# A recurrent layer's input projection as seven block products for eight, with the residual kept in DRAM

## The chip, the cores and the metric

The kernel runs on one core of a Trainium2 chip. The metric is the device time of one execution in microseconds (us). The time before is the median of three runs, 1123.8 us.

## The reference

Two pre-norm residual layers and a final RMSNorm over x of shape (1, 1024, 1024), all in float32. Layer 0 is a gated linear recurrence, layer 1 an attention with forget gates; the change touches layer 0 alone.

```python
h = rms_norm(x, norm_g[0])
u = h @ w_in                                  # (1024, 1024) @ (1024, 3072)
xb, gate = u[..., :1536], u[..., 1536:]
xc = causal_depthwise_conv(xb, conv_w, conv_b)        # 4 taps
r = sigmoid(block_diag_linear(xc, wa, ba))            # 12 blocks of 128 x 128
i = sigmoid(block_diag_linear(xc, wx, bx))
log_a = -8 * r * softplus(-a_param); a = exp(log_a)
hs = scan(a, sqrt(1 - a**2) * i * xc)                 # h[t] = a[t] h[t-1] + b[t]
x = x + (hs * silu(gate)) @ w_out                     # (1024, 1536) @ (1536, 1024)
# layer 1 (attention), then rms_norm
```

## The kernel before

Everything lies transposed: features on the 128 partitions, the 1024 positions along the free axis, cut into two halves of 512 (`halves`, index h). The model's 1024 features are eight blocks of 128 (k), and the recurrence's width of 1536 is twelve blocks (n). Each float32 operand of a product is split into a high part (`to_hi`, L85 or L87) and a low part, the rest (`to_lo`, L96), and each product of two blocks is three matmuls of 128x128 by 128x512: high by high, low by high, high by low (`gemm_steps`, all recorded at L54).

Layer 0 walks over the twelve blocks n. For each it needs two projections, `ups` (the value branch, weights `w0[n]`) and `gps` (the gate branch, weights `w0[12 + n]`), and each of these is eight blocks k by two halves h by three matmuls, so 48 matmuls and 96 for the pair. The split input lives in `raw[h][k]` throughout. The norm's reciprocal `rs` is multiplied in afterwards (L289, L323). Behind the projections come, for block n:

- `conv` (L289, L290, L293): `us` from PSUM, one ScalarE pass and three taps on VectorE, then the split of the result.
- `gates` (L314): 12 matmuls and four tanh on ScalarE.
- `silu` (L323 to L325) on `gps`; the projection of the gate branch and its silu run one block behind the value branch.
- `recur` (L339 to L348): tanh, exp, square and square root on ScalarE, a scan on VectorE (L348).
- `outputs` (L356): the product with the gate branch, and its split into `yh`, `yl`.

`project_out(g)` takes blocks 2g and 2g+1 back to the model's width: 16 results (8 feature blocks by 2 halves) of 6 matmuls each. VectorE adds each result from PSUM to the residual x, which is held in 16 SBUF tiles (L381). These results are the `fill`: the loop hands them out between the projections, four at a time. The last of the six groups runs after the loop, where each sum goes on at once into squares, into layer 1's split input (L247) and to DRAM as `x1d` (L475).

A scheduler orders the instructions of each engine at build time from this program; on the chip every engine then runs its own list strictly in that order, and so a waiting instruction holds up all that are behind it on its engine. PSUM has eight banks: the tag "S" has two slots of two banks (an `ups` or a `gps`), the tags "g" (results of the output projection) and "O" (gates) have two of one bank. Weights come in pieces of four blocks (256 KB) on SyncE's DMA queue through three `wf` buffers and one of four takes `wx`; the split weights have four `wh` and four `wl` buffers.

## Time and profile before

| | us |
|---|---|
| runs | 1123.17, 1123.8, 1128.24 |
| median | 1123.8 |
| span of the profiled execution | 1127.7 |
| TensorE matmuls busy | 1114.3 (99%) |
| VectorE, ScalarE, GpSimd busy | 758.6, 589.3, 195.6 |

The times do not mark which run the profile was taken from. Only 1128.24 can hold a span of 1127.7, so it is read as the profiled execution's own time: 0.5 us lie around the span.

The profile's page gives busy times by engine, the span in 40 slices, the chain of work that ended last, and groups of like instructions; further views give the same by stage or in order of time. PE is TensorE's matmuls, PEld its weight loads, DVE is VectorE, ACT is ScalarE, POOL is GpSimd, SP is SyncE. A matmul's recorded duration overlaps with that of its neighbours. The granted TensorE clock is given as a share of full speed.

### The profile page before, as it was taken

The page shows a single profiled execution, that of the slowest core. Times are in us where ns is not written, and L with a number is a line of the kernel's source. Part 1 is how long each engine was busy: PE and PEld are TensorE (multiplying, and loading weights), DVE is VectorE, ACT ScalarE, POOL GpSimd, SP SyncE. Part 2 cuts the span into 40 slices and gives each one's busy share as a digit, 9 for nine tenths or more (in the row PEclk, how much of TensorE's full clock was granted, in tenths as well). Part 3 has the DMA queues.
Part 4 walks back from the last instruction along what each step waited for, and adds up shares of the span by engine and source line. Part 5 has one row for each costly group of instructions (what it writes and reads, how often), then busy time and mean ns, then how long its engine had stood idle before and what let it go on. Part 6 is the DMA issues. An engine that isn't in the chain of part 4 may idle for free.

```text
span 1127.7 us, 15774 instructions
## 1 busy us (share of the span) xinstructions
PE 1114.3 (99%) x5691; PEld 936.8 (83%) x5691; DVE 758.6 (67%) x1268; ACT 589.3 (52%) x1081; POOL 195.6 (17%) x155
## 2 busy tenths in 40 slices
PE   9999999999999999999999999999999999999997
PEld 7788888888888887988888988889888898888786
DVE  7888755776568789656676466664667646676545
ACT  8488345355453656365555355553555535644335
POOL 1322112221121201431021110212102110021220
PEclk9999999999999999999999999999999999999999
DMA  6111111111111114433425224242252422564345
GB/s 235 57 47 42 51 52 52 38 58 45 52 38 52 47 44 145 129 112 102 112 71 123 66 77 117 72 118 71 74 119 73 118 71 77 176 189 158 117 154 187
DMA packets 62902, 105.43 MB, mean 93 GB/s; under 512 B 9796, under 2 KB 24772, under 8 KB 62824
## 3 DMA queue, kind: packets, MB, share of 16 engines
q1 hardware_dynamic: 59704, 95.97, 28.9%
q0 software_dynamic: 3120, 8.46, 2.3%
q8 instruction: 45, 0.74, 0.3%
q14 instruction: 33, 0.27, 0.1%
HBM read 63.30 MB, written 15.93 MB: 70 GB/s over the span
## 4 chain that ended last, share of the span: by engine, by line
PE 92%; DMA 2%; DVE 2%; issue 1%; ACT 1%; SPq 1%; POOL 0%; DVEq 0%; POOLq 0%; ACTq 0%
PE gps L54 33%; PE ops L54 16%; PE ups L54 12%; PE vps L54 8%; PE S L54 6%; PE O L54 6%; PE pt L58 5%; PE gate L54 3%; PE turn L54 3%; DMA wf<-in_wo 1%; DMA x<-in_xt 1%; POOL wl L96 0%; PE rsrow L54 0%; DMA wf<-in_w 0%; DMA yhl<-y1d 0%
## 5 line engine op out<-in xcount | busy, mean ns | idle before, releaser
L54 PE MATMUL gps<-hh,wh 128*128 128x512 f32 x576 | 229.1, 398 | 0.6 <-DVE qkl L595 0.6
L54 PE MATMUL gps<-hh,wl 128*128 128x512 f32 x576 | 226.8, 394 | 0.0
L54 PE MATMUL gps<-hl,wh 128*128 128x512 f32 x576 | 226.7, 394 | 0.0
L85 ACT CAST wh<-wf 128x512 fp32r<-128x512 f32 (+2 forms) x156 | 94.2, 607 | 147.8 <-PE ops L54 55.3
L96 POOL TENSOR_TENSOR wl<-wf,wh 128x512 fp32r<-128x512 f32 (+1 forms) x60 | 101.0, 1689 | 389.8 <-ACT wh L85 362.5
L720 ACT ACTIVATE p<-S,m 128x128 f32<-128x128 f32 (+7 forms) x128 | 94.8, 741 | 137.9 <-DVE m L715 136.8
L96 DVE TENSOR_TENSOR pl<-pt,ph 128x512 fp32r<-128x512 f32 (+1 forms) x198 | 98.7, 540 | 88.1 <-ACT ph L85 87.6
L54 PEld LDWEIGHTS gps<-hl,wh 128*128 128x128 f32 x576 | 108.3, 188 | 24.7 <-issue 0.5
L54 PEld LDWEIGHTS gps<-hh,wh 128*128 128x128 f32 x576 | 108.6, 189 | 20.5 <-DVE qkl L595 0.8
L54 PEld LDWEIGHTS gps<-hh,wl 128*128 128x128 f32 x576 | 108.7, 189 | 20.1 <-POOL wl L96 0.6
L715 DVE CUSTOM_DVE_ANT_0 S<-S,mask 128x128 f32<-128x128 f32 (+7 forms) x128 | 97.3, 761 | 28.8 <-PE S L54 28.8
L85 ACT CAST ph<-pt 128x512 fp32r<-128x512 f32 (+1 forms) x198 | 83.6, 473 | 36.2 <-PE pt L58 28.9
L54 PE MATMUL S<-T,U 96*128 96x512 f32 (+7 forms) x384 | 91.9, 348 | 2.7 <-ACT p L720 2.7
L96 DVE TENSOR_TENSOR wl<-wf,wh 128x512 fp32r<-128x512 f32 x96 | 70.7, 741 | 28.3 <-ACT wh L85 27.4
L381 DVE TENSOR_TENSOR x<-x,ops 128x512 f32<-128x512 f32 x80 | 54.1, 683 | 48.0 <-PE ops L54 48.0
L54 PEld LDWEIGHTS S<-T,U 128*128 128x128 f32 (+1 forms) x384 | 68.6, 190 | 16.1 <-ACT p L720 3.5
L58 PE MATMUL pt<-ident,p 128*128 128x128 f32 x576 | 79.4, 273 | 0.8 <-DVE pl L96 0.5
L58 PEld LDWEIGHTS pt<-ident,p 128*128 128x128 f32 x576 | 67.2, 140 | 13.9 <-issue 2.9
L54 PE MATMUL ups<-hh,wh 128*128 128x512 f32 x192 | 76.1, 397 | 1.1 <-ACT hh L87 1.1
L54 PE MATMUL ups<-hl,wh 128*128 128x512 f32 x192 | 76.7, 399 | 0.2
L54 PE MATMUL ops<-yh,wh 128*128 128x512 f32 x192 | 76.0, 396 | 0.5 <-DVE x L474 0.5
L54 PE MATMUL ups<-hh,wl 128*128 128x512 f32 x192 | 76.2, 397 | 0.0
(183 smaller groups left out, 2247.8 us busy)
## 6 DMA issues: line engine op xcount, KB each, us to landing
wf<-in_w SPq DMA_DIRECT2D x100, 256.0 KB
wf<-in_wo SPq DMA_DIRECT2D x64, 128.0 KB
U<-qkh SPq DMA_DIRECT2D x64, 128.0 KB
T<-qkh SPq DMA_DIRECT2D x28, 256.0 KB
x<-in_xt SPq DMA_DIRECT2D x16, 256.0 KB
x1d<-x SPq DMA_DIRECT2D x16, 256.0 KB
wf<-in_wv SPq DMA_DIRECT2D x16, 256.0 KB
U<-qkl SPq DMA_DIRECT2D x32, 128.0 KB
```

What stands on the lines that cost most here:

```text
L54: pe[0] = nc.tensor.matmul(*args, **kw)
L58: pe[0] = nc.tensor.transpose(*args)
L85: nc.scalar.copy(hi, src)
L96: return eng.tensor_tensor(lo, src, f32(hi), ALU.subtract)
L381: nc.vector.tensor_tensor(x, x, pt, ALU.add)
L715: nc.vector.tensor_tensor_reduce(S[:, :n], S[:, :n], mask[:, SEQ - n :], -1.0, -NEG, ALU.add, ALU.min, accum_out=m)
L720: seen[0] = nc.scalar.activation(p, S[:, :n], AF.Exp, bias=m, scale=-1.0, accum_out=sums[:, i : i + 1])
```

## The change

Blocks n = 3 to 11 no longer multiply eight times. With the two projections as the rows of a 2 by 2 block matrix (a11, a12 of `ups`, a21, a22 of `gps`, each half of the eight k) and the input's halves of k and of the positions as another, seven products of sums (12 matmuls each) take the place of eight, in a form of Strassen's scheme. The sums of the input (`other_sums`) are formed once, at n = 1 and 2, out of the x tiles, which they overwrite; the sums of the weights (`sums_of_weights`) are formed for each block on GpSimd. Three copies or sums pass between the PSUM banks on VectorE and ScalarE (`products`). Blocks 0 to 2 keep the eight products.

As the x tiles are consumed, x is copied from its input to `x1d` in DRAM at n = 2, and each result of the output projection is copied by ScalarE to an SBUF tile `o` (four buffers, shared with two tiles of `products`) and added to `x1d` by a DMA that GpSimd issues. After the loop the 16 x tiles are loaded again from `x1d`. The silu of a block now follows its own conv, the second gate's tanh comes first and is multiplied by `xc` in `gates`, `us` stays in PSUM, and several tiles have one buffer for two. The order of the fill is written out (`pace`). The scratch memory for DMA descriptors is set to 2048.

```diff
-GROUP = 2
+OUTS = 4
+PLAIN = 3
...
-        if spare and next(loads) % 4 == 3:
-            return spare[0].tile([P, *shape], F32, tag="wx", name="wf")
...
-        ypool = l0.enter_context(pool("y", 2 * GROUP))
+        early_x = l0.enter_context(ExitStack())
+        xpool = early_x.enter_context(pool("x", 1))
...
+        def split_pair(pair_, src, lo_eng):
+            hi, lo = pair_
+            to_hi(hi, src, nc.scalar)
+            to_lo(lo, src, hi, lo_eng)
+            return pair_
+        quad = {}
+        def other_sums(ks):
+            for k in ks:
+                lo_, hi_ = (gnt[:, 0, j : j + 1] for j in (k, k + 4))
+                t2, t3, n1, t4 = xs[0][k], xs[1][k + 4], xs[1][k], xs[0][k + 4]
+                nc.scalar.activation(t3, t3, AF.Copy, scale=hi_)
+                nc.scalar.activation(t2, t2, AF.Copy, scale=lo_)
+                stt = nc.vector.scalar_tensor_tensor
+                stt(t3, n1, lo_, t3, ALU.mult, ALU.subtract)
+                stt(n1, n1, lo_, t2, ALU.mult, ALU.subtract)
+                nc.vector.tensor_tensor(t2, t3, t2, ALU.subtract)
+                stt(t4, t4, hi_, t2, ALU.mult, ALU.add)
+                for key, src, eng in (("t2", t2, nc.vector), ("t3", t3, nc.gpsimd), ("n1", n1, nc.gpsimd), ("t4", t4, nc.gpsimd)):
+                    if key == "t4":
+                        to = pair()
+                    else:
+                        to = tuple(
+                            tpool.tile([P, HALF], F32R, tag=v, name=v, bufs=12) for v in ("th", "tl")
+                        )
+                    quad.setdefault(key, []).append(split_pair(to, src, eng))
+        def sums_of_weights(n):
+            def raw_w(block, k, tag, pool_=tmp):
+                wt = loaded([4, P]) if tag == "wf" else pool_.tile([P, 4, P], F32, tag=tag, name=tag, bufs=2)
+                nc.sync.dma_start(wt, w0[block][:, k : k + 4])
+                return wt
+            def split(src, lo_eng):
+                hi = wpool.tile([P, 4, P], F32R, tag="wh", name="wh")
+                lo = wpool.tile([P, 4, P], F32R, tag="wl", name="wl")
+                to_hi(hi, src, nc.scalar)
+                to_lo(lo, src, hi, lo_eng)
+                return [(hi[:, k], lo[:, k]) for k in range(4)]
+            def add(o, a, b):
+                nc.gpsimd.tensor_tensor(o, a, b, ALU.add)
+            a21, a22 = raw_w(NB + n, 0, "wx"), raw_w(NB + n, 4, "wx")
+            a11 = raw_w(n, 0, "wf")
+            s1, s2 = (tmp.tile([P, 4, P], F32, tag="ws", name="ws", bufs=2) for _ in range(2))
+            add(s1, a21, a22)
+            add(s2, s1, a11)
+            yield split(s2, nc.vector)
+            add(a21, a21, a11)
+            yield split(a21, nc.gpsimd)
+            yield split(a11, nc.gpsimd)
+            yield split(s1, nc.vector)
+            yield split(a22, nc.gpsimd)
+            a12 = raw_w(n, 4, "wf")
+            add(s2, s2, a12)
+            yield split(a12, nc.gpsimd)
+            yield split(s2, nc.vector)
+        def partial_sums(o, w, x, start):
+            for k, ((wh, wl), (xh, xl)) in enumerate(zip(w, x)):
+                for i, (a, b) in enumerate(((wh, xh), (wl, xh), (wh, xl))):
+                    matmul(o, a, b, start=start and k == i == 0, stop=k == 3 and i == 2, skip_group_check=not start)
+        def products(n, ups, gps):
+            sets = sums_of_weights(n)
+            p1, q5, q7, q6 = ups[:, 0], ups[:, 1], gps[:, 0], gps[:, 1]
+            w_, v5 = (ypool.tile([P, HALF], F32, tag="o", name=v, bufs=OUTS) for v in ("wk", "vk"))
+            tt = nc.vector.tensor_tensor
+            partial_sums(q6, next(sets), quad["t2"], True)
+            yield
+            partial_sums(q7, next(sets), quad["t3"], True)
+            yield
+            partial_sums(p1, next(sets), raw[0][:4], True)
+            nc.scalar.copy(w_, p1)
+            tt(w_, w_, q6, ALU.add)
+            tt(q7, q7, w_, ALU.subtract)
+            yield
+            partial_sums(q5, next(sets), quad["n1"], True)
+            nc.scalar.copy(v5, q5)
+            tt(q5, w_, q5, ALU.subtract)
+            tt(q6, q7, v5, ALU.add)
+            yield
+            partial_sums(q7, next(sets), quad["t4"], False)
+            yield
+            partial_sums(p1, next(sets), raw[0][4:], False)
+            yield
+            partial_sums(q5, next(sets), raw[1][4:], False)
+        def product(pt, h, w, ks=range(KT)):
+            gemm(pt, [(w[k], raw[h][k]) for k in ks])
 
         def conv(n, ups):
-            us, xc = long("us"), long("xc", bufs=2)
-            for pt, cs in zip(ups, halves if len(ups) == 2 else (slice(0, SEQ),)):
-                nc.vector.tensor_tensor(us[:, cs], pt, rs[:, cs], ALU.mult)
+            xc = long("xc")
+            if isinstance(ups, list):
+                us = long("m2")
+                for pt, cs in zip(ups, halves):
+                    nc.vector.tensor_tensor(us[:, cs], pt, rs[:, cs], ALU.mult)
+            else:
+                us = ups.rearrange("p a b -> p (a b)")
+                nc.vector.tensor_tensor(us, us, rs, ALU.mult)
             nc.scalar.activation(xc, us, AF.Identity, bias=cb[:, n : n + 1], scale=cw[3][:, n : n + 1])
...
-            for j, b_ in enumerate((hba, hbx)):
+            th, ti = s["t"] = long("th"), long("ti")
+            for j, b_ in ((1, hbx), (0, hba)):
+                if j:
+                    nc.vector.scalar_tensor_tensor(ti, ti, 1.0, s["xc"], ALU.add, ALU.mult)
...
+        def silu(s, gps):
             gs = gps.rearrange("p a b -> p (a b)")
-            sg = s["sg"] = long("sg")
-            for cs in parts:
-                g_, s_ = gs[:, cs], sg[:, cs]
-                nc.vector.tensor_tensor(g_, g_, rs[:, cs], ALU.mult)
-                nc.scalar.activation(s_, g_, AF.Tanh, scale=0.5)
-                nc.vector.scalar_tensor_tensor(s_, s_, 1.0, g_, ALU.add, ALU.mult)
-                yield
+            sg = s["sg"] = tmp.tile([P, SEQ], F32, tag="sg", name="sg", bufs=2)
+            nc.vector.tensor_tensor(gs, gs, rs, ALU.mult)
+            nc.scalar.activation(sg, gs, AF.Tanh, scale=0.5)
+            nc.vector.scalar_tensor_tensor(sg, sg, 1.0, gs, ALU.add, ALU.mult)
...
-            a, t = long("a", bufs=2), long("m2")
+            a, t = long("a"), long("m2")
...
-                        x = xs[h][db]
-                        nc.vector.tensor_tensor(x, x, pt, ALU.add)
+                        o = ypool.tile([P, HALF], F32, tag="o", name="o", bufs=OUTS)
+                        nc.scalar.copy(o, pt)
+                        nc.gpsimd.dma_start(x1d[h, :, db], o, accum_op=ALU.add)
...
+            if n >= PLAIN:
+                ups, gps = two_banks("ups"), two_banks("gps")
+                steps = products(n, ups, gps)
+                pace = {NB - 1: "00001100", NB - 2: "01011101"}.get(n, "11112011")
+                pace = iter(map(int, pace))
+                for _ in range(4):
+                    next(steps)
+                    take(fill, next(pace))
+                gates(n - 1)
+                take(fill, next(pace))
+                with tc.issue_after(state[n - 1]["last"].ins):
+                    outputs(n - 2)
+                if n % 2:
+                    fill = itertools.chain(fill, project_out((n - 3) // 2))
+                for _ in range(3):
+                    next(steps, None)
+                    take(fill, next(pace))
+            elif n:
+                wu, wn = (list(weights(w0[b])) for b in (n, NB + n))
+                with tc.issue_after(state[n - 1]["tap"].ins):
+                    other_sums(range(2 * n - 2, 2 * n))
+                if n == 2:
+                    early_x.close()
+                    ypool = l0.enter_context(pool("y", 3))
+                    nc.sync.dma_start(x1d, xt)
+                ups = [ps.tile([P, HALF], F32, tag="g", name="ups") for h in range(2)]
+                gps = two_banks("gps")
+                for h in (1, 0):
+                    product(ups[h], h, wu)
                 gates(n - 1)
                 if n > 1:
                     with tc.issue_after(state[n - 1]["last"].ins):
                         outputs(n - 2)
+                for h in (1, 0):
+                    product(gps[:, h], h, wn)
...
+            silu(state[n], gps)
...
+        outputs(NB - 2)
+        take(fill, 6)
         gates(NB - 1)
+        recur(NB - 1, halves)
         drain(fill)
...
+        xs = [[xpool.tile([P, HALF], F32, name=f"x{h}{k}") for k in range(KT)] for h in range(2)]
+        for h, k in itertools.product(range(2), range(KT)):
+            nc.sync.dma_start(xs[h][k], x1d[h, :, k])
...
+    nc = bacc.Bacc("TRN2", target_bir_lowering=False, num_devices=1, dynamic_dma_scratch_size=2048)
```

87 lines of the change are left out of this document (31 added, 56 removed).

## The prediction

> **What bounds the kernel now.** I read the page's busy times and slices first, then the stages by windows, then the chain of waits.
>
> ```profile
> span 1127.7 us, 15774 instructions
> PE 1114.3 (99%) x5691; PEld 936.8 (83%) x5691; DVE 758.6 (67%) x1268; ACT 589.3 (52%) x1081; POOL 195.6 (17%) x155
> PEclk9999999999999999999999999999999999999999
> ```
>
> ```profile
> 0.00:35.00 35.00, 32.67 (x127) 24.50 (x128) 24.56 (x35) 27.75 (x47) 8.14 (x12) 1.00 0.59 205
> 35.00:105.00 70.00, 70.00 (x304) 56.92 (x303) 66.14 (x74) 51.01 (x58) 17.69 (x10) 1.00 0.15 47
> 140.00:400.00 260.00, 260.00 (x1129) 212.08 (x1128) 177.56 (x183) 130.45 (x153) 49.48 (x29) 1.00 0.15 48
> 419.50:446.00 26.50, 25.89 (x119) 20.45 (x118) 24.65 (x43) 18.17 (x30) 2.60 (x2) 1.00 0.42 149
> ```
>
> The columns of the second fence are the stretch, its length, the busy time of PE, PEld, DVE, ACT and POOL (with counts), the granted clock, the DMA share and GB/s. Layer 0 runs to about 446 us. From 35 to 400 us PE has no idle time at all and its clock is full, so every matmul taken out of this stretch shortens the span, as long as the other engines keep up. DVE is the next one: 68% from 140 to 400 us, but 94% from 35 to 105 us and 93% at the layer's end. What one matmul costs is read from the chain (start, length, what):
>
> ```profile
> 35.09 19.39 PE ups L54 x84
> 411.39 14.60 PE ops L54 x63
> ```
>
> That is 19.39 / 84 = 0.231 and 14.60 / 63 = 0.232 us, not the recorded duration of about 0.39, which overlaps with the next.
>
> **What it removes.** Nine blocks with 7 x 12 = 84 matmuls for 96: 108 fewer, all 128x512. 108 x 0.232 = 25.0 us. Built programs bear the count out: 1620 `gps` matmuls for 1728, all other kinds unchanged; so that the product isn't made smaller is no rival.
>
> ```profile
> L54 PE MATMUL gps<-hl,wh 128*128 128x512 f32 x118 | 46.3, 392 | 0.0
> L54 PEld LDWEIGHTS gps<-hh,wl 128*128 128x128 f32 x118 | 22.2, 188 | 4.9
> ```
>
> The Trainium skill (Perfetto Trace Analysis, Identifying the Most-Contended Engine) says that matmul busy time misleads since matmuls are pipelined, and that the share of weight loads shows the headroom. Here that share is 212.08 / 260 = 82%, and by the loads alone the removed work would be 108 x 0.188 = 20.3 us; the trace agrees that 0.39 is not the price, but with PE's idle time at 0.0 the pitch is.
>
> **What it adds to the other engines in a block n = 4 to 10.** Durations from the groups of 140 to 400 us:
>
> ```profile
> L96 POOL TENSOR_TENSOR wl<-wf,wh 128x512 fp32r<-128x512 f32 x29 | 49.5, 1711 | 205.0 <-ACT wh L85 202.2 <-DVE x L381 2.7
> L381 DVE TENSOR_TENSOR x<-x,ops 128x512 f32<-128x512 f32 x58 | 39.2, 683 | 40.5 <-PE ops L54 40.5
> L85 ACT CAST wh<-wf 128x512 fp32r<-128x512 f32 x44 | 27.0, 617 | 66.4 <-PE ops L54 37.5 <-PE gps L54 13.5 <-issue 11.3
> L348 DVE TENSOR_TENSOR_SCAN a<-a,ti 128x1024 f32<-128x1024 f32 x7 | 19.7, 2812 | 0.2
> L314 ACT ACTIVATE th<-gate,hba 128x512 f32<-128x512 f32 x16 | 10.7, 688 | 23.3 <-PE gate L54 23.3
> L325 DVE SCALAR_TENSOR_TENSOR sg<-sg,gps 128x1024 f32<-128x1024 f32 x8 | 9.8, 1222 | 6.5 <-ACT sg L324 6.5
> L293 DVE SCALAR_TENSOR_TENSOR xc<-us,pct,xc 128x1022 f32<-128x1022 f32 x7 | 9.0, 1282 | 0.2
> L290 ACT ACTIVATE xc<-us,pct 128x1024 f32<-128x1024 f32 x7 | 8.7, 1246 | 2.0 <-DVE us L289 1.8
> L324 ACT ACTIVATE sg<-gps 128x1024 f32<-128x1024 f32 x8 | 8.2, 1024 | 3.6 <-DVE gps L323 3.6
> ```
>
> A block's PE time becomes 84 + 12 (gates) + 48 (fill) = 144 matmuls, 33.4 us (before 36.2).
> - DVE loses 8 residual adds (5.5 us) and gains 4 bank sums (2.7) and about 3 low parts (2.1): 24.6 us before (177.56 / 260 x 36.2), 24 after, 72%.
> - ACT gains 10 copies out of PSUM. No such copy is in the trace; between the cast (0.617) and the tanh from PSUM (0.688) I take 0.65, so 6.5 us, and 3 more casts (1.9): 18.2 before, 26.6 after, 80%.
> - POOL gets 4 weight sums and 4 low parts, 8 x 1.71 = 13.7 us, and 8 DMA issues:
>
> ```profile
> L879 POOL DMA_DIRECT2D x1d<-xp x16: 539/576/608, 993.5 to 1089.0; - x16
> DMA to landing us min/median/max: 2.3/3.4/5.7
> ```
>
> at 0.58 each 4.6, so 18.3 us, 55%. (These rows are plain writes of the same 256 KB from POOL; the accumulating form isn't in the trace.) All of it fits under 33.4 us. So the sum depends on chains, not on loads.
>
> **The chains.** Two slots of "S" now hold the pair for the whole block. In the built order, 45 matmuls (10.4 us) stand between the last one on `ups` of block 6 and the first on those banks for block 7; in them must pass `us` 1.22, ACT's pass 1.25, three taps at 1.28 and one low part 0.69, so 7.0, and an ACT copy ahead: about 3 us to spare. For `gps` there are 30 matmuls (7.0 us) for 1.22 + 1.02 + 1.22 + 0.69 = 4.2. Only the last two blocks, whose fill is kept for later, are tight: 32 matmuls (7.4) for 6.3 to 7.7, and 20 (4.6) for 3.5 to 4.8. I take 2 us lost here over all blocks; bounds 0 (all covered) and 9 (1 us in each of nine). A gain there isn't possible, since PE has no idle time to win.
>
> **The start.** Input sums put 20 more instructions of 128x512 on DVE (13.7 us) where it is at 94%, but the fill's adds and part of the later blocks' work go. In the built order DVE's queue from the second reciprocal on runs so:
>
> ```profile
> 32.51 0.39 PE L54 MATMUL gps<-hl,wh 128*128 128x512 f32 x1
> 36.63 3.35 DVE L275 RECIPROCAL rs<-rs 128x512 f32<-128x512 f32 x1
> 41.23 1.22 DVE L323 TENSOR_TENSOR gps<-gps,rs 128x1024 f32<-128x1024 f32 x1
> 42.36 0.16 DVE L210 TENSOR_TENSOR sp_e<-sp_e,sp_d 128x12 f32<-128x12 f32 x1
> ```
>
> An instruction of 1024 takes 42.36 - 41.23 = 1.13 of the queue; at 0.61 to 0.66 for 512 and 1.2 for a tap, the queue (28 of 512, 12 of 1024, 6 taps, a scan and small ones) reaches the silu of block 2 at 86 us if it never waits, and that of block 3 at 108. PE, counting its order from the last `gps` of block 0 (32.5), comes to the banks they free at 90 and 109. From 35 to 105 us DVE waited 70.00 - 66.14 = 3.9 us; with so much in waits PE would stand 0 and 3 us. I take 2; bounds 0 and 4.
>
> The copy of x to `x1d` (4.2 MB) stands in SP's queue ahead of weights for block 1. The first 35 us moved 205 GB/s at a DMA share of 0.59, so 347 at full: 12 us; if reads and writes both count against 205 GB/s, 41.
>
> ```profile
> 15.04 2.69 SPq L109 DMA_DIRECT2D wf<-in_w  x4
> 29.67 6.96 SPq L109 DMA_DIRECT2D wf<-in_w  x4
> 35.12 0.69 ACT L274 ACTIVATE rs<-rsrow,epst 128x512 f32<-128x512 f32 x1 [0.93 <-PE rsrow L54]
> ```
>
> It goes out behind the third `wf`, at about 17.7, and lands at 30 or 59. The next `wf` is issued at 29.7 and its cast stands on ACT right before the second half's norm (35.12 now). At 30 nothing is late, at 59 the norm, the conv and DVE's whole queue are 24 late and PE about 20. I take 30, at no cost, because the row that gives it is a like stream of loads.
>
> **The end.** The group after the loop is DVE's:
>
> ```profile
> 419.62 0.68 DVE L474 TENSOR_TENSOR x<-x,ops 128x512 f32<-128x512 f32 x1
> 439.86 1.68 PE sscol L54 x16
> ```
>
> Between them DVE does adds, squares and splits. After the change its fill is spent earlier: 57 matmuls (13.2 us) run from the last fill to `sscol`, while DVE has 23 instructions (14.6) and starts 1.2 later. 3 us lost; bounds 0 and 6. The reload of x waits for the last accumulations but is needed one by one.
>
> **Sum.** -25.0 + 2 + 2 + 3 = -18.0. On the profiled execution's 1128.2 that is 1110.2; the median of the runs lies 4.4 lower (1123.8), so I forecast 1105.8. Own range 1099 to 1113.
>
> **The rivals.**
> - *All covered.* The three losses are nothing: 1123.8 - 25 = 1099. For it: 3 us of slack in the regular blocks and no idle time in the same stretch before. Against it: DVE at 93 and 94% at both ends.
> - *POOL becomes the bound.* Its durations vary:
>
> ```profile
> 60.68 1.30 POOL L96 TENSOR_TENSOR wl<-wf,wh 128x512 fp32r<-128x512 f32 x1 [3.79 <-ACT wh L85]
> 75.60 3.43 POOL L96 TENSOR_TENSOR wl<-wf,wh 128x512 fp32r<-128x512 f32 x1 [13.63 <-ACT wh L85]
> ```
>
>  It decides from (33.4 - 4.6) / 8 = 3.6 us each; at 3.8 a block takes 35.0, 1.6 more, nine times 14: 1120, and at 3.9 35.8 and 1127. Against it: a mean of 1.71. The Trainium skill (SBUF — State Buffer, Who interferes with whom) says a VectorE instruction with two SBUF inputs contends with GpSimd's reads; by that rule the taps, whose `us` moves into PSUM, stop contending while POOL's work grows, and the mean would stay.
> - *The accumulating DMA is slow* (the slower side). Ten tiles of a block share four `o` buffers; a buffer may be held 4 x 33.4 / 10 = 13.4 us on average, and with `wk`, `vk` short, an `o` about 15.7. Copy, POOL's queue and issue take about 3, so it decides from a landing of 12.5 us. Beyond it ACT waits in its queue, then the banks of "g", then PE: 8 / 4 = 2 us a block for each us. At 16 us (the worst plain landing, 5.7, nearly threefold): 2 x 3.5 x 9 = 63, so 1106 + 63 = 1169; it ends slower than before from about 13.8 us (1106 + 23), and I price it at 14.5: 1106 + 36 = 1142. For it: read and write per element at DRAM, unseen here. Against it: 3.4 us now.
> - *The copy holds the weights back*: 1106 + 20 = 1126.
>
> **Chances.** Forecast 0.53, all covered 0.15, POOL 0.12, slow accumulation 0.12, copy 0.08. 0.5% is about what a measurement of this kernel can tell from no change, 5.6 us. Faster (below 1118.2): 0.68 and half of POOL's, 0.74. Same: the other half and the copy's, 0.14. Slower: 0.12. The range from 1098 (25.0 and half a us of PE's idle time at 419.5 to 446) to 1126 leaves out the slow accumulation and little else.
>
> **What would show it.** Right: 108 matmuls fewer, PE idle under 1 us a block from 130 to 380 us, layer 1 starting about 18 us earlier, `o` landing under 6 us, ACT near 80%. Wrong: PE idle before the first matmul of each `ups` or `gps` (chains), ACT idle before an `o` on a DMA (accumulation), POOL's mean over 3 us, or PE waiting at 40 to 60 us for `wf` (copy).

## The result, and the profile after

The changed kernel took 1154.5 us (median of 4 runs, 1153.17 to 1155.41) beside 1123.9 us for the kernel before (4 runs, 1123.17 to 1128.24): a ratio of 1.027, interval 1.0248 to 1.0288. It is slower, which was not forecast, and 48.7 us above the forecast of 1105.8. Its profiled execution took 1154.09 us with a span of 1152.3.

The profile of the changed kernel, page: span, busy times, the granted clock in slices.

```profile
span 1152.3 us, 16120 instructions
PE 1107.5 (96%) x5583; PEld 920.1 (80%) x5583; DVE 798.9 (69%) x1270; ACT 661.5 (57%) x1227; POOL 339.1 (29%) x283
PEclk9997999999999999999999999999999999999999
```

PE has 5691 - 5583 = 108 matmuls fewer, as the change says. But it is busy for only 6.8 us less, where 25.0 were counted on, and idle in 4% of the span for 1% before. And one slice of the clock is at 7. Where that is shows in the windows of the changed kernel (stretch, its length, busy time and count of PE, PEld, DVE, ACT and POOL, clock, DMA share, GB/s):

```profile
35.00:70.00 35.00, 35.00 (x148) 27.48 (x147) 33.00 (x35) 14.18 (x20) 18.58 (x13) 1.00 0.15 48
70.00:105.00 35.00, 25.49 (x89) 18.70 (x87) 34.41 (x35) 20.19 (x28) 22.72 (x13) 0.85 0.07 19
105.00:140.00 35.00, 24.96 (x89) 18.96 (x90) 31.39 (x31) 23.93 (x29) 15.31 (x8) 0.82 0.15 45
140.00:180.00 40.00, 37.10 (x153) 29.75 (x152) 26.67 (x24) 26.11 (x37) 20.64 (x18) 0.95 0.54 100
180.00:360.00 180.00, 179.75 (x775) 145.19 (x774) 141.27 (x129) 124.54 (x173) 99.93 (x83) 1.00 0.59 112
360.00:420.00 60.00, 56.52 (x237) 43.60 (x236) 45.09 (x47) 41.72 (x58) 26.64 (x24) 1.00 0.52 99
420.00:440.00 20.00, 19.10 (x79) 14.19 (x78) 10.79 (x10) 18.40 (x28) 8.33 (x10) 1.00 1.07 222
440.00:460.00 20.00, 15.77 (x60) 10.80 (x61) 18.34 (x28) 12.72 (x24) 4.35 (x5) 1.00 1.09 309
```

Three things are to be seen. In the middle, 180 to 360 us, PE has no idle time, as forecast. From 70 to 140 us it stands 9.51 + 10.04 = 19.55 us, and what it does there is slow: 178 matmuls in 50.45 us are 0.283 each, where the prediction's row gives 0.231; at 0.232 they would take 41.3, so the halved clock costs another 9. DVE is full in the same stretch (34.41 of 35) and POOL has 22.72 us of work where it had 10.37 before. Then, from 360 us on, PE stands again, and from 420 us the DMA share is above 1: the recorded times of the packets add up to more than the 16 engines' time in the stretch. The chain of waits of the changed kernel shows both the half clock and the regular block (start, length, what):

```profile
111.60 5.47 PE ups L55 x12
...
212.32 5.60 PE gps L55 x24
...
245.77 5.60 PE gps L55 x24
...
279.24 5.59 PE gps L55 x24
```

The last three stand 33.45 and 33.47 us apart: a block takes the 33.4 us that were predicted. The first takes 5.47 / 12 = 0.456 us for each matmul, right behind the longest wait of PE between 35 and 150 us (waits of PE in the changed kernel: sum, times, longest, us):

```profile
PE ups L55 <- DVE sg L420: 7.2, 1, 7.2
PE gate L55 <- ACT xch L86: 3.4, 1, 3.4
```

The first is the wait for the banks that the silu of block 2 frees, the very one that the prediction's part on the start had counted through DVE's queue.

**A marker.** The 16 `sscol` matmuls that follow the first half of the positions in layer 0 start at 439.70 us before and at 463.55 after: 23.85 of the span's 24.6 us more (1152.3 - 1127.7) are lost ahead of them. From the marker to the end of the span the profiled executions take 688.0 us in before, 688.8 in after and 687.2 to 690.7 in the experiments below, but 683.2 in e3 and 683.4 in e11. These two lack a wait in layer 1 that the profiles of all others show between 1045 and 1080 us (PE for `p` of ScalarE, 1.9 to 2.9 us). So a median can carry about 5 us that layer 0 has no part in, and a difference of medians may differ from one of markers by as much. The profiled execution of before lay 4.4 us above its median; whether its faster runs lack this wait no profile shows.

### The profile page after: what moved, and what is told of

Same layout as the page of the kernel before. It is cut to its first block, busy times and chain, and to the rows that moved or that the text cites. A ratio compares the mean times of both kernels' runs of the same rounds, so it can differ in the third digit from the quotient of the medians.

```text
span 1152.3 us, 16120 instructions
## 1 busy us (share of the span) xinstructions
PE 1107.5 (96%) x5583; PEld 920.1 (80%) x5583; DVE 798.9 (69%) x1270; ACT 661.5 (57%) x1227; POOL 339.1 (29%) x283
## 4 chain that ended last, share of the span: by engine, by line
PE 74%; DVE 9%; issue 7%; DMA 3%; ACT 3%; POOL 3%; SPq 0%; POOLq 0%; ACTq 0%; DVEq 0%
PE gps L55 26%; PE ops L55 11%; PE ups L55 8%; PE vps L55 8%; PE S L55 6%; PE O L55 6%; PE pt L59 5%; PE turn L55 3%; POOL x1d L481 2%; POOL wl L97 1%; PE gate L55 1%; DVE xc L388 1%; DMA x1d<-o 1%; DMA wf<-in_w 1%; DMA wf<-in_wf 1%
## 5 line engine op out<-in xcount | busy, mean ns | idle before, releaser
L55 PE MATMUL gps<-hh,wh 128*128 128x512 f32 x468 | 187.4, 401 | 1.2 <-DVE qkl L709 1.0
L55 PE MATMUL gps<-hl,wh 128*128 128x512 f32 x468 | 185.1, 395 | 0.0
L55 PE MATMUL gps<-hh,wl 128*128 128x512 f32 x468 | 185.0, 395 | 0.0
L55 PEld LDWEIGHTS gps<-hl,wh 128*128 128x128 f32 x468 | 88.3, 189 | 20.2
L481 POOL DMA_DIRECT2D x1d<-o x80 | 71.7, 950 | 103.2 <-ACT o L480 102.4
L55 PEld LDWEIGHTS gps<-hh,wh 128*128 128x128 f32 x468 | 88.5, 189 | 16.9 <-DVE qkl L709 1.2
L55 PEld LDWEIGHTS gps<-hh,wl 128*128 128x128 f32 x468 | 88.7, 190 | 15.7 <-POOL wl L97 0.2
L97 POOL TENSOR_TENSOR wl<-wf,wh 128x512 fp32r<-128x512 f32 (+1 forms) x42 | 68.9, 1644 | 95.9 <-ACT wh L86 74.3
L55 PE MATMUL ups<-hh,wh 128*128 128x512 f32 x156 | 64.4, 414 | 9.9 <-DVE sg L420 7.2
L55 PE MATMUL vps<-wh,hh 128*128 128x256 f32 (+1 forms) x256 | 72.5, 286 | 0.7 <-DVE qkl L97 0.5
```

Source lines behind the costliest of these rows:

```text
L55: pe[0] = nc.tensor.matmul(*args, **kw)
L97: return eng.tensor_tensor(lo, src, f32(hi), ALU.subtract)
L481: nc.gpsimd.dma_start(x1d[h, :, db], o, accum_op=ALU.add)
```

## The experiments

In the expectations the theories bear letters. A: at the start, DVE's instructions grow longer because POOL works beside them. B: DVE simply has too many of them there. C: the copy of x to `x1d` makes block 1 late. D: the accumulating DMAs fill the DMA engines at the end. E: at the end the chain of the last blocks has too little other work beside it. F: the pace at which the fill is spent decides the end. What the runs gave, with the marker of each profiled execution. Each ratio is to runs of before that were made beside that kernel (medians 1123.59 to 1124.81):

| kernel | median us (lowest to highest, runs) | ratio to before, interval | marker us |
|---|---|---|---|
| before | 1123.9 (1123.17-1128.24, 4) | | 439.70 |
| after | 1154.51 (1153.17-1155.41, 4) | 1.0268 [1.0248, 1.0288] | 463.55 |
| e1_shared_low | 1146.26 (1143.76-1148.77, 2) | 1.0204 [1.0150, 1.0258] | 456.33 |
| e2_no_sums | 1126.30 (1124.76-1128.28, 8) | 1.0022 [1.0004, 1.0040] | 434.08 |
| e3_eight | 1141.13 (1138.21-1144.05, 2) | 1.0158 [1.0096, 1.0221] | 453.00 |
| e4_no_accum | 1147.48 (1146.71-1148.24, 2) | 1.0215 [1.0185, 1.0244] | 457.49 |
| e5_low_dve | 1146.86 (1144.99-1148.73, 2) | 1.0198 [1.0150, 1.0246] | 455.35 |
| e6_pace | 1154.66 (1154.14-1155.17, 2) | 1.0268 [1.0238, 1.0297] | 463.96 |
| e7_start | 1136.25 (1136.19-1136.30, 2) | 1.0104 [1.0075, 1.0133] | 446.25 |
| e8_both | 1138.52 (1138.49-1138.55, 2) | 1.0124 [1.0095, 1.0153] | 449.37 |
| e9_plain4 | 1136.59 (1134.27-1138.68, 4) | 1.0104 [1.0085, 1.0122] | 444.44 |
| e10_end2 | 1130.45 (1126.80-1131.74, 7) | 1.0043 [1.0029, 1.0057] | 439.71 |
| e10b_direct | 1135.32 (1134.04-1136.49, 4) | 1.0093 [1.0078, 1.0108] | 441.79 |
| e11_eight_no_accum | 1130.27 (1129.81-1130.49, 3) | 1.0044 [1.0026, 1.0061] | 445.27 |
| e12_late_fill | 1126.70 (1125.03-1128.62, 12) | 1.0012 [0.9999, 1.0025] | 436.50 |

**e1 to e4: the change taken apart.** The four are edits of the changed kernel. In e1, `t3`, `n1` and `t4` take the low part of `t2` and have none of their own:

```diff
-                    quad.setdefault(key, []).append(split_pair(to, src, eng))
+                    if key == "t2":
+                        lo2 = split_pair(to, src, eng)[1]
+                    else:
+                        to_hi(to[0], src, nc.scalar)
+                    quad.setdefault(key, []).append((to[0], lo2))
```

e2 makes no sums of x and multiplies by a part of x as it is:

```diff
-            for k in ks:
...
+            for key in ("t2", "t3", "n1", "t4"):
+                quad[key] = raw[1][4:]
```

e3 has e2's edit and eight half products in place of seven, so that it has all matmuls of before:

```diff
-            sets = sums_of_weights(n)
...
+            wn, wu = weights(w0[NB + n]), weights(w0[n])
+            for k in (0, 4):
+                for pt, src in ((gps, wn), (ups, wu)):
+                    w = list(itertools.islice(src, 4))
+                    for h in range(2):
+                        partial_sums(pt[:, h], w, raw[h][k : k + 4], k == 0)
+                        if k == 0 or pt is gps:
+                            yield
```

e4 leaves the accumulation of the output projection into `x1d` out:

```diff
-                        nc.gpsimd.dma_start(x1d[h, :, db], o, accum_op=ALU.add)
```

> Leaves out the 12 low parts of the input sums that GpSimd forms (t3, n1, t4); the low part of t2 stands in for them, so TensorE and VectorE have the same instructions as in the changed kernel. Theory A (collisions: a VectorE instruction that reads both operands from SBUF while GpSimd works takes about 1.1 us more; in the changed kernel some 20 of them, 23 us, between 44 and 111 us, of which about 11 fall on these low parts): the STTs of the sums that now take 1.78 us come down to about 0.7 where no weight part runs beside them, the silu of block 2 ends at about 98 us for 111, and the time falls by 12 to 20 us, to 1135 to 1143. Theory B (VectorE's queue is too long by its own 20 added instructions, whatever GpSimd does): the same durations, the silu at 110, 1151 to 1156.

> Leaves out the input sums altogether (scaling on ScalarE, sums on VectorE, their splits); the parts of the input itself stand in for them, TensorE does the same matmuls. Both theories A (collisions) and B (VectorE's own queue) expect the start's loss of about 34 us to go nearly whole: the 24 matmuls of block 5's first two products start at about 146 to 150 us for 178.9, and the time is 1120 to 1128. Theory C (the start is late because of the copy of x and of the weights behind it): no more than 5 us are won, 1149 or more.

> The residual in DRAM alone: all eight block products as in the kernel before, in the order of the changed one, and no sums of inputs or weights; the sequence of fills, the copies to o and the accumulating DMA stay. Theory A or B (the start's loss comes from the sums) with an end that loses about 15 us whatever the products: 1123.8 + 12 to 16, so 1134 to 1142, PE full from 35 to 350 us with 36.2 us a block. If the end's loss belongs to the short blocks of seven products instead (gates and banks with less cover): 1122 to 1128.

> Leaves out the 80 accumulating DMAs (the copies to o stay, so the residual misses these products). Theory D (from 410 to 455 us the DMA engines are full, and buffers of o and the reloaded x come late): the loss between 347 us and layer 1 falls by 5 to 8 us, 1146 to 1150. Theory E (the waits there are those of the gates and of DVE's chain with little fill beside them, not of the transfers): within 3 us of 1154.

e2 came out as A and B expected, and C fell with it: the copy stands in e2 at its place (issued at 17.40 us), and the norm's second root starts at 35.36, where it was at 35.12 before. The markers, each of one execution, split the change into three steps, each between two neighbours:

- before to e3, 439.70 to 453.00: the residual in DRAM, and the order that goes with it, with all 96 matmuls kept: +13.3.
- e3 to e2, 453.00 to 434.08: seven products for eight, with the sums of weights and in the banks: -18.9.
- e2 to after, 434.08 to 463.55: the sums of the input: +29.5.

In medians the three are +17 (1141.13 - 1123.9), -15 and +28. So the removed matmuls are worth most of what was counted, and the two other parts together cost more than twice that.

e1 leaves out 12 of POOL's low parts and nothing that DVE does. The step from the end of the second reciprocal to the end of the silu of block 2, through DVE's queue, fell from 67.7 us to 57.6, and the run by 8: a part of A, and less than the 12 to 20 expected. In its profile the second reciprocal ended late as well, 46.3, for 43.7 after. e3 came out in its first range (1134 to 1142): an end that loses whatever the products are. The windows of e3 and then of before show where it loses (columns as above):

```profile
360.00:400.00 40.00, 40.00 (x175) 32.57 (x174) 25.79 (x25) 22.35 (x30) 10.94 (x11) 1.00 0.49 89
400.00:440.00 40.00, 34.57 (x142) 25.75 (x141) 25.78 (x32) 33.10 (x52) 14.82 (x17) 1.00 1.07 223
```

```profile
400.00:440.00 40.00, 39.39 (x171) 31.07 (x169) 35.70 (x56) 21.59 (x34) 0.00 (x0) 1.00 0.25 86
```

PE of e3 has no idle time from 35 to 395 us, so what its DMAs, copies and new order cost is lost behind that, where the DMA share stands at 1.07 instead of 0.25. e4, the changed kernel without the accumulation, is 7.0 us faster in the median and 6.1 at the marker, as D had expected (1146 to 1150).

**e5: DVE's count or POOL's company.** All low parts of the sums go to DVE, 12 instructions more for it:

```diff
-                for key, src, eng in (("t2", t2, nc.vector), ("t3", t3, nc.gpsimd), ("n1", n1, nc.gpsimd), ("t4", t4, nc.gpsimd)):
+                for key, src, eng in (("t2", t2, nc.vector), ("t3", t3, nc.vector), ("n1", n1, nc.vector), ("t4", t4, nc.vector)):
```

> Moves the 12 low parts of the input sums (t3, n1, t4) from GpSimd to VectorE; everything is still computed. Theory A (collisions, 1.1 us each): VectorE's queue from the end of the second reciprocal to the end of the silu of block 2, 67.8 us in the changed kernel, loses about 11 collisions (12 us) and gains 11 to 12 instructions of 0.62 (7 us): 62 to 65, and the time is 2 to 8 us shorter, 1147 to 1152. Theory B (VectorE's queue is too long by its own work): 7 us are added and none taken, 75 us and 1158 to 1165.

DVE's queue between the same two points became shorter, 62.3 us for 67.7, with more in it, and the run 7.6 us faster. B is refuted, A confirmed. Between the two points 22 instructions of DVE in the changed kernel are more than 0.4 us longer than the shortest of their kind, 11 in e1 and 10 in e5. What A is, in the timeline of the changed kernel (start, length, engine, line, what):

```profile
89.22 6.72 POOL L97 TENSOR_TENSOR tl<-x,th 128x512 fp32r<-128x512 f32 x4 [5.20 <-ACT th L86]
89.63 3.48 DVE L299 SCALAR_TENSOR_TENSOR x<-x,gnt,x 128x512 f32<-128x512 f32 x2
...
93.03 3.46 DVE L97 TENSOR_TENSOR tl<-x,th 128x512 fp32r<-128x512 f32 x2
...
96.41 2.29 DVE L440 TENSOR_TENSOR ti<-ti,m 128x1024 f32<-128x1024 f32 x1
```

and in that of e1, where POOL has no low part to do at this point:

```profile
85.90 1.40 DVE L299 SCALAR_TENSOR_TENSOR x<-x,gnt,x 128x512 f32<-128x512 f32 x2
87.22 1.28 DVE L97 TENSOR_TENSOR tl<-x,th 128x512 fp32r<-128x512 f32 x2
89.90 1.23 DVE L444 TENSOR_TENSOR ti<-ti,m 128x1024 f32<-128x1024 f32 x1 [1.40 <-ACT m L443]
```

The same instruction takes 3.48 / 2 = 1.74 us beside POOL and 0.70 without, the low part 1.73 and 0.64, the one of 1024 elements 2.29 and 1.23. Each time it is about 1.05 us more, whatever the size. Where this amount comes from can be read in layer 1 of the kernel before, where an instruction of POOL is longer:

```profile
564.75 2.39 POOL L747 TENSOR_TENSOR sg<-sg,recb 64x1024 f32<-64x1024 f32 x1 [4.28 <-DMA recb<-recd]
565.49 2.19 DVE L96 TENSOR_TENSOR wl<-wf,wh 128x512 fp32r<-128x512 f32 x1 [1.42 <-ACT wh L85]
```

POOL ends at 567.14 and DVE at 567.68, 0.5 us later, and a low part of this size takes 0.68 alone. DVE's instruction has waited until POOL's was over and then done its own work; here that cost 1.5 us. The 22 in the changed kernel end in the same way, each a time that goes with its own size after one of POOL's (0.55 us at 512 elements, 1.08 at 1024). POOL's instructions are all of one size there and stand close behind one another, and so the wait is much the same each time. The groups of DVE from 44 to 112 us in the changed kernel (busy, mean ns, idle before) show which kinds are hit:

```profile
L296 DVE SCALAR_TENSOR_TENSOR x<-x,gnt,x 128x512 f32<-128x512 f32 x4 | 7.1, 1784 | 0.0
...
L381 DVE TENSOR_TENSOR m<-ups,rs 128x512 f32<-128x512 f32 x6 | 3.8, 656 | 0.0
L418 DVE TENSOR_TENSOR gps<-gps,rs 128x1024 f32<-128x1024 f32 x3 | 3.7, 1219 | 0.0
...
L92 DVE CAST wgh<-wgf 128x256 fp32r<-128x256 f32 x2 | 2.7, 1368 | 0.0
...
L209 DVE TENSOR_SCALAR sp_q<-sp_d 128x12 f32<-128x12 f32 x1 | 1.3, 1269 | 0.0
```

Those with an operand in PSUM (`ups`, `gps`) kept their time: 656 ns and 1219 ns. Of those with all operands in SBUF many did not; even one of 12 elements took 1.27 us, where the prediction's row of that size has 0.16. 22 of DVE's instructions in this stretch were longer than their kind, by 22.6 us in sum. Not every meeting costs DVE something: at 76.44 us a tap began first and kept its 1.28 us, and POOL's addition, begun at 76.60, took 2.27 us, where one took 1.26 at 34.98. The Trainium skill (SBUF — State Buffer, Who interferes with whom) says that a VectorE instruction with two SBUF inputs contends with a GpSimd instruction that reads SBUF, that casts and tensor_scalar can contend in some modes, and that the order of issue decides who blocks; the trace agrees with which kinds are hit and with waits on both sides, and the 1.05 us are this case's measurement.

**e6: the pace of the fill.**

```diff
-                pace = {NB - 1: "00001100", NB - 2: "01011101"}.get(n, "11112011")
+                pace = {NB - 1: "11112011", NB - 2: "11112011"}.get(n, "11112011")
```

> Spends the output projections of blocks 10 and 11 at the pace of the other blocks (8 tiles each for 5 and 2), so 14 tiles are left for the end and not 23. Theory F (the end is late because y of block 9 finds no free buffer until the third last group of projections is drained, which the slow pace puts behind the last block; the recurrences of 10 and 11 then come late, and with them all that follows): y of block 9 is written at about 390 us and not 413, and the time falls by 4 to 10 us. Theory D (the DMA engines are full at the end): a fall of 2 to 6 us, since transfers start earlier. Theory E (too little fill beside the last chain): no gain or a loss, 1153 to 1162.

Nothing came of it (1154.66). Its windows:

```profile
360.00:420.00 60.00, 60.00 (x260) 48.59 (x259) 47.96 (x48) 43.41 (x61) 29.20 (x26) 1.00 0.66 120
420.00:440.00 20.00, 17.19 (x70) 12.38 (x68) 9.78 (x9) 17.50 (x26) 6.95 (x8) 1.00 1.09 270
440.00:460.00 20.00, 12.33 (x40) 8.54 (x41) 17.73 (x26) 10.63 (x19) 1.73 (x2) 0.83 0.76 224
```

PE is full up to 420 us, where it stood 3.5 us in the changed kernel, and then stands 10.5 us up to 460 us, where it stood 5.1, with a lower clock. The `yh` of block 9 did come earlier, at 399.49 us for 412.96, and it gained nothing: F is refuted, the loss only moved. D had expected 2 to 6 us here and missed too; E had this range.

**e7: the start without the collisions.** x lies in tiles of 1024, ScalarE does all scalings, DVE adds whole pairs and does all low parts; what block 2 doesn't need comes behind its silu, and the softplus ahead of the second half's split:

```diff
+            for x, k0 in ((t3, 2 * j + 4), (n1, 2 * j), (t2, 2 * j), (t4, 2 * j + 4)):
+                for i in range(2):
+                    nc.scalar.activation(x[:, i], x[:, i], AF.Copy, scale=gnt[:, 0, k0 + i : k0 + i + 1])
+            tt = nc.vector.tensor_tensor
+            tt(t3, n1, t3, ALU.subtract)
+            tt(n1, n1, t2, ALU.subtract)
+            tt(t2, t3, t2, ALU.subtract)
+            tt(t4, t4, t2, ALU.add)
+            def split_sum(key, src):
+                to = tuple(tpool.tile([P, 2, HALF], F32R, tag=v, name=v, bufs=6) for v in ("th", "tl"))
+                split_pair(to, src, nc.vector)
...
+            if n == 2:
+                with tc.issue_after(state[n]["done"].ins):
+                    rest()
```

> Start rearranged, the same results: the input sums as instructions of 128x1024 (scaling of all four inputs on ScalarE, behind the pass of the conv, so no longer ahead of the norm), all low parts on VectorE, the last ones behind the silu of block 2, and the 18 small softplus instructions ahead of the norm. Theory A: VectorE's queue from the second reciprocal to the end of the silu of block 2 takes 52 to 58 us for 67.8, with about 8 collisions left; the second reciprocal ends at about 41 us for 43.7; the time falls by 16 to 24 us, 1130 to 1138. If the loss at the start were the clock's or the copy's: no more than 5 us.

The run fell by 18 us to 1136.25, the marker by 17.3. The second reciprocal ends at 39.95 again and DVE's queue to the silu of block 2 takes 56.9 us. Part of the loss stayed; PE still waits 3.7 us for that silu, and its clock is still low for a while (windows of e7):

```profile
70.00:105.00 35.00, 27.87 (x106) 21.32 (x105) 33.40 (x32) 25.20 (x33) 11.87 (x7) 0.85 0.13 38
105.00:140.00 35.00, 30.50 (x130) 23.84 (x129) 30.69 (x28) 26.57 (x34) 13.68 (x9) 1.00 0.26 58
```

**e8: e7, and the end without accumulation.** The tiles of the second last output projection are added on DVE to an x that is loaded back at the end of the loop:

```diff
+                        if g == NB // 2 - 2:
+                            nc.vector.tensor_tensor(xs[h][db], xs[h][db], pt, ALU.add)
+                            yield
+                            continue
...
+        sums_.close()
+        xpool = l0.enter_context(pool("x", 1))
+        xs = [[xpool.tile([P, HALF], F32, name=f"x{h}{k}") for k in range(KT)] for h in range(2)]
+        for k, h in itertools.product(range(KT), range(2)):
+            nc.sync.dma_start(xs[h][k], x1d[h, :, k])
```

> The start of the run before this one, and another end, the same results: blocks 10 and 11 at the pace of the others, the buffers of the sums are given to x after the last block, x is read back then, and the last group of projections that goes beside the chain is added to it by VectorE, so 64 accumulating DMAs for 80 and 16 copies less on ScalarE. Theories D and F: the end's loss falls by 8 to 12 us more, 1118 to 1128. Theory E: no more than 3 us better than the start alone.

A miss for D and F: 2.3 us slower than e7. The DMA share from 395 to 431 us is 0.30, but PE is busy for 29.97 of these 36 us. It waits 5.7 us in four places for the additions to x, which stand in DVE's queue between the conv, the scan and the outputs of blocks 10 and 11 (DVE is busy for 30.34 of the 36). That is as E has it. With the DMA share down and E in its place, e8 alone couldn't tell what D is worth.

**e9: one block fewer with sums at the start.** Block 3 is taken as a plain product too, with two tiles of fill, so nothing of the sums is wanted before block 4:

```diff
-PLAIN = 3
+PLAIN = 4
...
+                if n > 2:
+                    with tc.issue_after(state[n - 1]["last"].ins):
+                        outputs(n - 2)
+                    fill = project_out(0)
...
                     product(gps[:, h], h, wn)
+                    if n > 2:
+                        take(fill, 1)
```

> The rearranged start (wide sums on VectorE, softplus early), and block 3 with eight products too, so seven products in 8 blocks for 9; same results. One more block of eight costs 12 matmuls, 2.8 us. Theory A (VectorE's queue is about 8 us late when block 3 first needs both slots of banks): with eight products block 3 needs the second slot 25 us later, VectorE catches up, TensorE's idle time from 70 to 150 us falls from about 12 us to under 5, and the slow clock after the idle time goes: 3 to 9 us better than the rearranged start alone, 1127 to 1133. If what is left there is not VectorE's lateness: 1139, the 2.8 us worse.

A miss as well: 1136.59 with 12 matmuls more than e7. Windows of e9:

```profile
70.00:105.00 35.00, 35.00 (x153) 28.38 (x152) 30.00 (x27) 23.37 (x28) 9.77 (x6) 1.00 0.12 38
105.00:140.00 35.00, 28.83 (x113) 21.67 (x111) 25.75 (x24) 24.61 (x32) 16.00 (x12) 0.95 0.36 73
```

The start is whole up to 105 us, for the first time with sums in the kernel. Then the first output tiles wait: 2.9 us for copies of `ops` on ScalarE, 2.1 for DVE to read the banks of `ups` (`m`), 1.8 for `yh`. The loss moved from block 2 to block 4.

**e10, e10b, e11: what the accumulation costs at the end.** e10 is e9 with half of the last tiles added on DVE, each x tile loaded just ahead, and the last block's products in another order; blocks 10 and 11 also spend their fill earlier, as in e8. e10b adds both halves on DVE. e11 is e3 without the accumulating DMAs.

Of e10_end2, from e9:

```diff
+            last = [(q7, quad["t4"]), (p1, raw[0][4:]), (q5, raw[1][4:])]
+            if n == NB - 1:
+                last = last[1:] + last[:1]
...
+                        if g == NB // 2 - 2 and h == 0:
+                            nc.sync.dma_start(xs[h][db], x1d[h, :, db])
+                            nc.vector.tensor_tensor(xs[h][db], xs[h][db], pt, ALU.add)
+                            yield
+                            continue
```

e10b_direct, from e10, and e11_eight_no_accum, from e3:

```diff
-                        if g == NB // 2 - 2 and h == 0:
+                        if g == NB // 2 - 2 and True:
...
-                        nc.gpsimd.dma_start(x1d[h, :, db], o, accum_op=ALU.add)
```

> The run before this one, and another end, same results: the last block finishes the banks of its conv first, 14 instead of 23 tiles of the output projection are left after it is issued plus the last group, and of that group the first half of the sequence is added by VectorE to x read back tile by tile, the second half goes through ScalarE and accumulating DMA (72 for 80). Theory E (the end is set by the chain of the last two blocks, which lacks matmuls beside it) : no more than 4 us won over the run before. Theory D (transfers at the end): 5 to 10 us won, 1118 to 1126.

> As the run before, with both halves of the last group added by VectorE to x read back tile by tile (64 accumulating DMAs for 80, none after block 11). Theory D: 1 to 4 us better than the half. Theory E: 0 to 3 us worse, since VectorE's chain gets eight more adds of 0.6.

> Eight products and the residual in DRAM, as in the earlier run with eight products, but the 80 accumulating DMAs are left out (the residual misses these products). That run was 17 us above the kernel before, all of it lost after 395 us. Theory D (accumulations and reload fill the DMA engines from 395 to 450 us): 10 to 15 us are won back, 1126 to 1131. Theory E: under 5 us, 1136 or more.

e11 won 10.9 us over e3 in the median, 7.7 at the marker: D. (The two runs of e3 lie 5.8 us apart, so the marker is the better figure.) e10 won 6.1 over e9, in D's range; it changes three things at once, of which e6 had shown that the earlier fill alone gains nothing. Taking the second half off the DMAs as well (e10b) gave 4.9 back, with a DMA share of 0.22 from 400 to 440 us and PE busy for 34.2 of 40: E again, and more than the 0 to 3 expected. The DMA view of e3 from 395 to 455 us tells D's price (queue, packets, MB, share of 16 engines; q0 carries the accumulating DMAs, q1 the plain ones):

```profile
q0 software_dynamic: 3119, 5.67, 60.3%
q1 hardware_dynamic: 5029, 8.39, 39.7%
```

The accumulating queue took 0.603 x 60 = 36.2 us of all 16 engines for 5.67 MB, 1.67 us for a tile of 256 KB; the plain one 0.397 x 60 = 23.8 for 8.39 MB, 0.74 a tile. The crowd at the end is not what makes the difference: from 180 to 360 us of e3, at shares of 40.5% and 15.9% for 9.96 and 8.53 MB, the same working gives 1.92 and 0.88. Nor is it POOL's queue: in before, from 985 to 1092 us, that queue carried 4.99 MB without accumulation (16 of its tiles plain writes to `x1d`) at 13.4%, which is 0.75 a tile. Some 22 accumulations after 395 us are then 36 us of DMA work, and the reload of x, 16 x 0.74 = 12, stands behind them. What is late for it, in the timeline of e3:

```profile
443.83 0.69 DVE L557 TENSOR_TENSOR x<-x,ops 128x512 f32<-128x512 f32 x1 [2.98 <-DMA x<-x1d]
```

**e12: the fill later.** From e10, the two tiles of block 3 move into block 4:

```diff
-                pace = {NB - 1: "11112000", NB - 2: "11112011"}.get(n, "11112011")
+                pace = {NB - 1: "11112000", NB - 2: "11112011", 4: "22112011"}.get(n, "11112011")
...
-                    if n > 2:
-                        take(fill, 1)
```

> The half-and-half end and eight products in blocks 1 to 3, as before, but the first two tiles of the output projection move from block 3 to block 4 (same results). In the run with them in block 3 TensorE waited there for banks and for y of block 1 (about 8 us idle from 105 to 150 us, and a clock of 0.95 after it). If those waits are the fill's place, as the waits of that trace say, 5 to 9 us are won, 1121 to 1126, and TensorE is full from 105 to 180 us. If VectorE's lateness is behind them (theory A's queue not caught up), the waits go over to the banks of block 4, and no more than 2 us are won.

1126.70, 3.8 us won, between the two ranges, with a ratio to before of 1.0012 (0.9999 to 1.0025): the loss of the change is undone, and nothing more. At the marker e12 is 3.2 us ahead of before. From there to the end its profile takes 688.3 us beside 688.0, but the faster runs of before lie 4.4 us below the one that was profiled, so the lead doesn't come out in the medians. PE stands 6.3 us between 105 and 140 (3.2 on copies of `ops`) and 6.4 between 360 and 440. No run takes these two away, and no version was found that beats the kernel before. Counted in matmuls, 34 of the 96 that e12 has fewer are lost from 105 to 140 us (PE does 119, before did 153), 9 from 140 to 180 and 8 from 180 to 360. That is 51 x 0.232 = 11.8 us of the 22.3 that the 96 are worth; with the 3.2 of the marker, about 7.3 are left, and they go from 360 us on.

## Why the prediction was wrong, point by point

**Right.** The removed matmuls (108), the pitch, the period of a block (33.45 us for 33.4), and that nothing waits in the regular blocks: 0.25 us of idle time in 180. Two of the loads there were near the estimates, POOL 99.93 / 180 = 56% for 55 and DVE 78% for 72; ACT had 69% for 80. The groups of the changed kernel from 180 to 360 us for two prices that had no row before:

```profile
L480 ACT COPY o<-ops 128x512 f32<-128x512 f32 x40 | 23.6, 589 | 1.7 <-PE ops L55 1.0 <-DMA x1d<-o 0.4
...
L441 DVE TENSOR_TENSOR_SCAN a<-a,ti 128x1024 f32<-128x1024 f32 x6 | 22.5, 3744 | 0.2
```

The copy took 0.59 for the 0.65 taken. The scan shows that DVE is hit here too: 3.74 us in the mean for 2.81 before. With DVE at 78% it costs nothing; an extra us is harmless in a stretch with slack and costs itself in one without. The copy of x to `x1d` cost nothing (e2, e3), as taken.

**The start: the step that failed.** "I take 2; bounds 0 and 4" came from 28 instructions of 512 "at 0.61 to 0.66", 12 of 1024 and 6 taps, a queue that "reaches the silu of block 2 at 86 us if it never waits". From the second reciprocal at 40 that is 46 us. Without the 22.6 us of lengthening the measured queue is 67.7 - 22.6 = 45.1: the count was right, and the durations weren't. They were taken from rows beside which POOL had little work (17.69 us from 35 to 105), while the change itself put 12 low parts and more on POOL there (41.3 us). The timeline of before already holds the collision, at one of the few places where POOL works:

```profile
43.71 1.36 POOL L96 TENSOR_TENSOR wl<-wf,wh 128x512 fp32r<-128x512 f32 x1 [7.44 <-ACT wh L85]
43.83 1.27 DVE L212 TENSOR_SCALAR sp_q<-sp_d 128x12 f32<-128x12 f32 x1
```

The rule on the shared port was in the prediction, but it was asked only what DVE does to POOL's durations. B falls with e5, and e1, e5 and e7, each of which takes POOL's work away in another manner, all win 7.6 to 18 us (e7 with the order of the norm mended too).

A second, smaller part: the queue began 3.7 us late. The timeline of the changed kernel:

```profile
27.98 0.71 ACT L293 ACTIVATE x<-x,gnt 128x512 f32<-128x512 f32 x1
...
31.20 1.95 ACT L293 ACTIVATE x<-x,gnt 128x512 f32<-128x512 f32 x3
...
37.96 0.69 ACT L271 ACTIVATE rs<-rsrow,epst 128x512 f32<-128x512 f32 x1 [0.52 <-PE rsrow L55]
...
40.39 3.35 DVE L272 RECIPROCAL rs<-rs 128x512 f32<-128x512 f32 x1
...
110.25 1.21 DVE L420 SCALAR_TENSOR_TENSOR sg<-sg,gps 128x1024 f32<-128x1024 f32 x1
```

Four scalings of the first sums stand in ScalarE's queue ahead of the norm that everything waits for, and the second root comes at 37.96 for 35.12 before. The prediction had costed the sums on DVE and never laid out ScalarE's order ahead of them. Both together bring the silu of block 2 to 111.5 us for 86; by the prediction's count PE needed it at 90, and of the 29.5 us that the sums cost, 24 show by 140 us: from 35 us on PE did 326 matmuls, e2 430, and 104 x 0.232 is 24.1.

**The end: mis-sized, by a resource left out.** "3 us lost; bounds 0 and 6" counted DVE's instructions against the fill. The part of the change that was charged to it, the residual in DRAM, cost 13.3 at the marker (e3), of which the accumulation is 7.7 (e11). Of the other 5.6, PE's idle time in e11 shows 4.2 from 400 to 440 us, at a DMA share of 0.22, mostly behind the copies `o` on ScalarE and the additions to x on DVE; no run separates these two. The rival on slow accumulation had weighed only the landing against a threshold of 12.5 us. The rows of the changed kernel on `x1d` (issue time min, median, max in ns; landing in us):

```profile
L481 POOL DMA_DIRECT2D x1d<-o x80: 858/872/1562, 146.7 to 448.4; - x80
...
DMA to landing us min/median/max: 2.3/4.9/7.9
```

The landing stayed below the threshold, and the issue, 0.87 us for the 0.58 taken, fits into POOL's time. That rival, too, was about the regular blocks: its place was wrong, since what decided is how much DMA time a tile takes when the last 22 of them meet the reload of the whole x. "The reload of x waits for the last accumulations but is needed one by one" named the collision and gave it no price.

**The chains: 2 taken, 6 measured.** Between e3 and e2 18.9 of the 25.0 us came out. The window of e2 in which the most of it is lost:

```profile
70.00:105.00 35.00, 31.08 (x130) 23.77 (x129) 29.27 (x25) 23.75 (x30) 11.23 (x7) 1.00 0.14 42
```

3.9 us of idle time where the sevenfold products begin, not in the last blocks as the prediction looked for it; from 360 to 440 us e2 stands 7.6 us, e3 5.4, so some of it is there too. This lies within the bound of 9; it was the size that was off, and the place.

By the marker the three steps together are (29.5 - 2) + (13.3 - 3) + (6.1 - 2) = 41.9 us, which is what lies between 463.55 and the 439.7 - 18 = 421.7 that the sum would give. Of the other 6.8 us of the miss, 4.4 are what the profile of before lies above its median.

**The rivals.** "POOL becomes the bound" had the right engine in sight, but POOL was never the bound; it slowed the one that was. No rival had its collision with DVE in the place where DVE was at 94%.

## What to carry to other kernels

Where an engine is near full in a stretch, price what the change adds there with the durations of that engine beside the new neighbours: work sent to GpSimd to spare VectorE can cost VectorE more than doing it itself (e5), up to the length of a GpSimd instruction each time. A transfer that is hidden in the steady state has a second price, its share of the DMA engines, which falls due where the last transfers meet a reload that others wait for. And a matmul taken out of a PE that is 100% busy is worth its pitch only as long as the chains around it have as much slack as it took away.

## What the runs showed of the hardware

Where an instruction of DVE with its operands in SBUF began during one of POOL's, it waited for that one to end and then took its own time. With POOL's instructions of 128x512 close behind one another that cost about 1.05 us whatever DVE's size: 0.16 to 1.27 us at 12 elements, 0.70 to 1.74 at 512, 1.23 to 2.29 at 1024, 2.29 to 3.26 for a scan of 1024 (at 98.74 us of the changed kernel). Behind an instruction of POOL of 2.39 us it cost 1.5. Begun in the other order, it was POOL's that grew (1.26 to 2.27 us). Instructions with an operand in PSUM kept their time.

An accumulating DMA took 2.3 times the DMA time of a plain one for the same bytes (1.67 and 0.74 us of 16 engines for 256 KB; 2.2 times in the regular blocks of e3), 0.87 us to issue for 0.58, and a median of 5.0 us to land on the page's list of DMA issues for 3.4.

The half clock followed even a short stop. Timeline of PE in e10, after an idle time of 2.13 us:

```profile
116.70 0.50 PE L55 MATMUL ops<-yh,wh 128*128 128x512 f32 x1 [2.13 <-DVE m L393]
...
118.14 0.63 PE L55 MATMUL gate<-xcl,wgh 128*128 128x512 f32 x1
118.56 0.63 PE L55 MATMUL ops<-yh,wh 128*128 128x512 f32 x1
```

The matmuls come 0.43 us apart from 118.14 to 120.70, for 0.23 before. So a wait of PE costs more than its length here. What the clock alone adds (the 9 us of the start) is worked out from the trace, and no run took it away by itself.
